# Query-key scores for 96 heads: float32 loads on the store queue with casts on GpSimd, in place of casting loads

## The chip, the cores and the metric

The kernel runs on one core of one Trainium2 chip. Its time is the device time of one execution, in microseconds. Differences of a few tenths of a per cent count here, so the profile of one execution is read beside the median of several.

## The reference

For 8 batches of 12 heads, every query row is multiplied with every key row. There is no scale, no mask and no softmax:

```
q, k: (8, 12, 1024, 64) float32
out = np.einsum('bhid,bhjd->bhij', q, k)      # (8, 12, 1024, 1024) float32
```

The inputs are 25.2 MB each, and the output is 402.7 MB. A head is one (1024 x 64) by (64 x 1024) product with 4 MB of output.

## The kernel before

The 96 heads are taken in batches of 1, 1, 2 and then 4 heads. For each batch, GpSimd's queue loads q and k from float32 in memory into float16 tiles (line 64); the DMA engines cast on the way. Three batches are loaded ahead and there are four input buffers.

A load of G heads puts 8 x G consecutive rows of the batch in each partition. TensorE transposes these rows through an identity (lines 78, 81, 82) so that the 64 head dimensions lie on partitions: for q, two tiles of rows side by side in one 128-column transpose; for k, each tile twice, to partitions 0-63 and 64-127, so that it meets either half of q. One such group, 4 + 16 transposes, goes to one PSUM tile (`t_ps`), and VectorE copies it out, q by head (line 91) and k in one copy (line 92).

`scores` makes one head: eight tiles of 128 query rows, each two products of 64 x 128 with 64 x 512 into a PSUM tile of two banks (`ps`, line 106; three such tiles). Tiles 1, 4 and 6 are evacuated by VectorE (line 112), the other five by ScalarE (line 114), into the head's output tile `o_sb` of 32 KB a partition. There are four of these. When all eight tiles are in, SP's queue stores the head in one 4 MB transfer (line 115), 32 KB per partition. A fifth head can therefore not be evacuated until the first one's store has landed.

Between the heads of a batch, the next batch is transposed. The order of instructions on each engine is set by the scheduler of the framework, which moved some products between the transposes; the queue of SP carries stores alone, and the queue of GpSimd carries loads alone.

Of the kernel before, what the change touches and what calls it, by code (L numbers as in the profile page):

```python
# [1 line left out]

# [5 lines left out]


F16 = mybir.dt.float16  # L10
F32 = mybir.dt.float32
P = 128


@with_exitstack
def kernel(
    ctx: ExitStack,
    tc: tile.TileContext,
    q: bass.AP,
    k: bass.AP,  # L20
    out: bass.AP,
):
    nc = tc.nc

    B, H, S, D = q.shape
    NT = S // P
    BH = B * H
    GMAX = 4
    assert D == 64 and NT == 8 and BH % GMAX == 0

    qf = q.rearrange("b h s d -> (b h s) d")
    kf = k.rearrange("b h s d -> (b h s) d")
    of = out.rearrange("b h i j -> (b h) i j")

    sizes = [1, 1, 2] + [GMAX] * (BH // GMAX - 1)
    assert sum(sizes) == BH  # L40

    consts = ctx.enter_context(tc.tile_pool(name="consts", bufs=1))
    ident = consts.tile([P, P], F16)

    in_pool = ctx.enter_context(tc.tile_pool(name="in_pool", bufs=4))
    tr_pool = ctx.enter_context(tc.tile_pool(name="tr_pool", bufs=2))
    out_pool = ctx.enter_context(tc.tile_pool(name="out_pool", bufs=4))
    pt_pool = ctx.enter_context(
        tc.tile_pool(name="pt_pool", bufs=1, space=bass.MemoryType.PSUM)
    )  # L50
    po_pool = ctx.enter_context(
        tc.tile_pool(name="po_pool", bufs=3, space=bass.MemoryType.PSUM)
    )

    class Batch:
        def __init__(self, first, G):
            self.first, self.G, self.R = first, G, 8 * G

        def load(self):
            rows = slice(self.first * S, (self.first + self.G) * S)  # L60
            self.q_sb = in_pool.tile([P, GMAX * NT, D], F16, tag="q")
            self.k_sb = in_pool.tile([P, GMAX * NT, D], F16, tag="k")
            for src, dst in ((qf, self.q_sb), (kf, self.k_sb)):
                nc.gpsimd.dma_start(  # L64
                    out=dst[:, : self.R],
                    in_=src[rows].rearrange("(p r) d -> p r d", p=P),
                )

        def alloc(self):
            self.qT = tr_pool.tile([P, GMAX * 4 * P], F16, tag="qT")  # L70
            self.kT = tr_pool.tile([P, GMAX * S], F16, tag="kT")

        def transpose(self, a):
            G, pp = self.G, P // self.G
            t_ps = pt_pool.tile([P, 12, P], F16, tag="pt")
            for e in range(4):
                r = a * NT + 2 * e
                nc.tensor.transpose(t_ps[:, e], self.q_sb[:, r : r + 2], ident)  # L78
            for t in range(NT):
                rows = self.k_sb[:, a * NT + t]  # L80
                nc.tensor.transpose(t_ps[0:64, 4 + t], rows, ident)  # L81
                nc.tensor.transpose(t_ps[64:128, 4 + t], rows, ident)  # L82
            qT = self.qT[:, : G * 4 * P].rearrange(
                "c (g e m a) -> c g e m a", g=G, e=4, m=pp
            )
            kT = self.kT[:, : G * S].rearrange(
                "c (g m a t) -> c g m a t", g=G, m=pp, t=NT
            )
            for g in range(G):
                ms = slice(g * pp, (g + 1) * pp)  # L90
                nc.vector.tensor_copy(out=qT[:, g, :, :, a], in_=t_ps[:, 0:4, ms])  # L91
            nc.vector.tensor_copy(  # L92
                out=kT[:, :, :, a],
                in_=t_ps[:, 4:12].rearrange("c t (g m) -> c g m t", g=G),
            )

        def scores(self, g):
            bh = self.first + g
            qT = self.qT.rearrange("c (g e m) -> c g e m", e=4, m=P)
            kT = self.kT.rearrange("c (g j) -> c g j", j=S)  # L100
            o_sb = out_pool.tile([P, NT, S], F32, tag="out")
            for t in range(NT):
                h = (t % 2) * 64
                ps = po_pool.tile([P, S], F32, tag="po")
                for n in range(2):
                    nc.tensor.matmul(  # L106
                        ps[:, n * 512 : (n + 1) * 512],
                        qT[h : h + 64, g, t // 2],
                        kT[h : h + 64, g, n * 512 : (n + 1) * 512],
                    )  # L110
                if t in (1, 4, 6):
                    nc.vector.tensor_copy(out=o_sb[:, t], in_=ps)  # L112
                else:
                    nc.scalar.copy(out=o_sb[:, t], in_=ps)  # L114
            nc.sync.dma_start(
                out=of[bh].rearrange("(p t) j -> p (t j)", p=P),
                in_=o_sb.rearrange("p t j -> p (t j)"),
            )

    batches, first = [], 0  # L120
    for G in sizes:
        batches.append(Batch(first, G))
        first += G

    AHEAD = 3
    for b in batches[:AHEAD]:
        b.load()
    make_identity(nc, ident)
    batches[0].alloc()
    for a in range(batches[0].G):  # L130
        batches[0].transpose(a)
    for i, b in enumerate(batches):
        if i + AHEAD < len(batches):
            batches[i + AHEAD].load()
        nxt = batches[i + 1] if i + 1 < len(batches) else None
        if nxt:
            nxt.alloc()
        for g in range(b.G):
            b.scores(g)
            if nxt:  # L140
                for a in range(g * nxt.G // b.G, (g + 1) * nxt.G // b.G):
                    nxt.transpose(a)


# [1 line left out]
_INS = ['q', 'k']  # L146
_OUTS = [((8, 12, 1024, 1024), 'float32')]


# [23 lines left out]
```

## Time and profile before

| what | value |
|---|---|
| median of 10 runs | 1071.07 us (1070.06 to 1071.59) |
| the profiled execution | 1071.11 us |
| span of its instructions | 1069.3 us |
| TensorE products and transposes, busy | 626.5 us, 3456 |
| VectorE busy | 566.0 us, 758 instructions |
| ScalarE busy | 468.5 us |
| GpSimd busy | 28.4 us |
| stores | 96 of 4 MB, median 36.6 us from issue to landing |
| casting loads | 52 |

The span is the time from the first to the last instruction in the profile. "Busy" is the time in which an engine executes; a share below one means that it waits for something. The time from issue to landing of a transfer includes its wait behind earlier transfers. The lines of the profile that carry the argument are shown in the prediction.

### The profile page before, as it was taken

To read this page: it belongs to the slowest core of one execution; us is meant where nothing else is said; L and a number is where in the kernel's file an instruction comes from. 1 tells how busy PE (TensorE), PEld (TensorE's weight loads), DVE (VectorE), ACT (ScalarE), POOL (GpSimd) and SP (SyncE) were. 2 spreads that over 40 slices of the span, in tenths; PEclk is the share of its full clock that TensorE was granted. 3 is DMA by queue.
4 is the path that set the end of the run, shared out by engine and by line. 5 is a ranking of instruction groups with operands and counts; after the bars stand their busy time and mean duration, and the time that the engine had idled before them with its cause. 6 is when DMAs were issued, how large, how long until landed. Compare 5 with 4: busy or idle time off the path is not lost.

```text
span 1069.3 us, 8844 instructions
## 1 busy us (share of the span) xinstructions
PE 626.5 (59%) x3456; PEld 213.2 (20%) x3456; DVE 566.0 (53%) x758; ACT 468.5 (44%) x481; POOL 28.4 (3%) x58
## 2 busy tenths in 40 slices
PE   6786565574755646556465565655655567667530
PEld 2222121121221212212122121121211212212100
DVE  5676455464554645536456465564654656655420
ACT  4454453444434444444444434444344445454530
POOL 3000000000000000000000000000000000000000
PEclk9985555555555555555555555555555555555555
DMA  9999999999999999999999999999999999999996
GB/s 203 389 386 391 391 406 415 387 421 401 402 420 389 417 402 398 419 389 415 406 398 423 386 409 409 398 423 387 409 410 398 421 434 430 430 430 431 431 433 288
DMA packets 21353, 428.39 MB, mean 401 GB/s; under 512 B 2368, under 2 KB 2880, under 8 KB 9024
## 3 DMA queue, kind: packets, MB, share of 16 engines
q1 hardware_dynamic: 13824, 402.66, 88.0%
q0 software_dynamic: 7488, 25.17, 11.9%
q8 instruction: 27, 0.44, 0.1%
q14 instruction: 14, 0.11, 0.0%
HBM read 50.33 MB, written 402.65 MB: 424 GB/s over the span
## 4 chain that ended last, share of the span: by engine, by line
DMA 77%; PE 7%; ACT 7%; DVE 1%; issue 0%; ACTq 0%
DMA out_dram<-o_sb 77%; ACT o_sb L114 7%; PE ps L106 6%; DVE kT L92 0%; DVE qT L91 0%; PE t_ps L81 0%; PE t_ps L78 0%; DVE o_sb L112 0%; PE t_ps L82 0%; ACTq L114 0%
## 5 line engine op out<-in xcount | busy, mean ns | idle before, releaser
L114 ACT COPY o_sb<-ps 128x1024 f32<-128x1024 f32 x480 | 467.2, 1014 | 566.2 <-DMA out_dram<-o_sb 345.4
L106 PE MATMUL ps<-kT,qT 64*128 64x512 f16 x1536 | 479.1, 595 | 272.6 <-ACT o_sb L114 228.8
L112 DVE COPY o_sb<-ps 128x1024 f32<-128x1024 f32 x288 | 352.0, 1224 | 372.1 <-DMA out_dram<-o_sb 210.2
L106 PEld LDWEIGHTS <-qT 64*128 64x128 f16 x1536 | 99.8, 109 | 604.1 <-issue 579.4
L91 DVE COPY qT<-t_ps 128x128 f16<-128x128 f16 (+1 forms) x374 | 121.3, 469 | 97.1 <-PE t_ps L82 97.0
L78 PE MATMUL t_ps<-ident,q_sb 128*128 128x128 f16 x384 | 56.7, 300 | 135.3 <-DVE kT L92 129.6
L92 DVE COPY kT<-t_ps 128x1024 f16<-128x1024 f16 x96 | 118.8, 1238 | 0.0
L81 PE MATMUL t_ps<-ident,k_sb 128*64 128x128 f16 x768 | 103.1, 312 | 0.0
L82 PE MATMUL t_ps<-ident,k_sb 128*64 128x128 f16 x768 | 102.9, 312 | 0.0
L81 PEld LDWEIGHTS <-k_sb 128*64 128x64 f16 x768 | 77.9, 166 | 19.9 <-issue 19.5
L82 PEld LDWEIGHTS <-k_sb 128*64 128x64 f16 x768 | 77.7, 165 | 8.4 <-issue 8.4
L78 PEld LDWEIGHTS <-q_sb 128*128 128x128 f16 x384 | 34.7, 127 | 187.9 <-issue 121.9
L64 POOL DMA_DIRECT2D q_sb<-in_q_dram x26 | 14.0, 539 | 767.0 <-PE t_ps L78 766.2
L64 POOL DMA_DIRECT2D k_sb<-in_k_dram x26 | 13.9, 536 | 13.2 <-PE t_ps L82 13.1
L114 ACT ACT_TABLE_LOAD x1 | 1.3, 1283 | 0.7 <-PEq L157 0.7
masks.py:199 POOL TENSOR_SCALAR_AFFINE_SELECT ident<-ident 128x128 f16<-128x128 f16 x1 | 0.4, 357 | 0.0
masks.py:197 POOL MEMSET ident<- 128x128 f16 x1 | 0.3, 267 | 0.0
L157 POOL MEMSET const-float32-0.0<- 128x1 f32 x1 | 0.1, 99 | 0.2 <-issue 0.2
L157 POOL MEMSET const-bfloat16-1.0<- 128x1 bf16 x1 | 0.1, 102 | 0.0
L157 POOL MEMSET const-uint8-127<- 128x1 uint8 x1 | 0.1, 102 | 0.0
L157 POOL MEMSET const-float32-1.0<- 128x1 f32 x1 | 0.1, 99 | 0.0
## 6 DMA issues: line engine op xcount, KB each, us to landing
out_dram<-o_sb SPq DMA_DIRECT2D x96, 4096.0 KB, 36.6
q_sb<-in_q_dram POOLq DMA_DIRECT2D x23, 512.0 KB, 17.9
k_sb<-in_k_dram POOLq DMA_DIRECT2D x23, 512.0 KB, 29.2
q_sb<-in_q_dram POOLq DMA_DIRECT2D x2, 128.0 KB, 3.6
k_sb<-in_k_dram POOLq DMA_DIRECT2D x2, 128.0 KB, 3.7
q_sb<-in_q_dram POOLq DMA_DIRECT2D x1, 256.0 KB, 5.1
k_sb<-in_k_dram POOLq DMA_DIRECT2D x1, 256.0 KB, 5.8
```

The lines of the kernel that those rows point to most:

```text
L64: nc.gpsimd.dma_start(out=dst[:, : self.R], in_=src[rows].rearrange("(p r) d -> p r d", p=P),)
L78: nc.tensor.transpose(t_ps[:, e], self.q_sb[:, r : r + 2], ident)
L81: nc.tensor.transpose(t_ps[0:64, 4 + t], rows, ident)
L82: nc.tensor.transpose(t_ps[64:128, 4 + t], rows, ident)
L91: nc.vector.tensor_copy(out=qT[:, g, :, :, a], in_=t_ps[:, 0:4, ms])
L92: nc.vector.tensor_copy(out=kT[:, :, :, a], in_=t_ps[:, 4:12].rearrange("c t (g m) -> c g m t", g=G),)
L106: nc.tensor.matmul(ps[:, n * 512 : (n + 1) * 512], qT[h : h + 64, g, t // 2], kT[h : h + 64, g, n * 512 : (n + 1) * 512],)
L112: nc.vector.tensor_copy(out=o_sb[:, t], in_=ps)
L114: nc.scalar.copy(out=o_sb[:, t], in_=ps)
L157: nc = _bacc.Bacc("TRN2", target_bir_lowering=False, num_devices=1)
```

## The change

Heads are taken in blocks of 2, 2, 4 and then 8, each in two halves of 1, 1, 2 and 4 heads. Each block is loaded in four pieces: q and k of the first half, q and k of the second. The pieces are plain float32 transfers, into three input buffers of 8 KB a partition. GpSimd casts each piece to float16 and places the two halves side by side in one block buffer (`half_sb`, one buffer): 64 columns of the first half, 64 of the second. One 128 x 128 transpose thus puts the first half's head dimensions on partitions 0-63 and the second half's on 64-127, for q and for k alike. A group is 8 transposes of q or 8 of k, to a PSUM tile of one bank (two of these), and one VectorE copy.

All instructions are held in the order in which they are written (`pin`). The transposes of the next block are written into the scores of the current one: q's after tile 1 and k's after tile 6, for as many heads as the next block has in a half.

At the start, the pieces of the first three blocks go to an output tile that is not yet in use, and three of the fourth block's pieces to the input buffers, from SP's and ScalarE's queues in turn. Later pieces are issued on SP's queue between the stores. `refill` does it: after the last head that transposes the next block, it casts three pieces of the block after that, loads and casts the fourth, and loads the first piece of yet another block; the other two follow after later heads. In the last block, two of the four pieces are cut by partition into several transfers.

```diff
-    in_pool = ctx.enter_context(tc.tile_pool(name="in_pool", bufs=4))
+    in_pool = ctx.enter_context(tc.tile_pool(name="in_pool", bufs=3))
+    half_pool = ctx.enter_context(tc.tile_pool(name="half_pool", bufs=1))
...
+            cuts = (0, P)
+            if self.first + 2 * self.G == BH and n < 2:
+                cuts = ((0, 112, 120, 124, 126, 127, P), (0, 112, 119, 124, 127, P))[n]
+            for lo, hi in zip(cuts, cuts[1:]):
+                pin(eng.dma_start(out=raw[lo:hi], in_=src[lo:hi]))
...
+        def cast(self, n):
+            pin(
+                nc.gpsimd.tensor_copy(
+                    out=self.halves[n % 2][:, :, n // 2],
+                    in_=self.raw[n].rearrange("p (r d) -> p r d", d=D),
+                )
+            )
...
+            for t in range(NT):
+                rows = self.halves[x][:, a * NT + t]
+                pin(nc.tensor.transpose(t_ps[:, t], rows, ident))
...
+                if t in side:
+                    side[t]()
...
+    for b in blocks[:3]:
+        for n in range(4):
+            piece = raw[:, 2 * at + n * b.elems :][:, : b.elems]
+            b.load(n, (nc.sync, nc.scalar)[n % 2], piece)
+        b.place(half_sb, at)
+        at += 2 * b.elems
+    for n in range(3):
+        blocks[3].load(n, (nc.sync, nc.scalar)[n % 2])
...
+    def refill(i):
+        b = blocks[i] if i < len(blocks) else None
+        c = blocks[i + 1] if i + 1 < len(blocks) else None
+        if b:
+            half_sb = half_pool.tile([P, 2 * half_elems], F16, tag="half")
+            b.place(half_sb, 0)
+            for n in range(3):
+                b.cast(n)
+            b.load(3, nc.sync)
+            b.cast(3)
+        if c:
+            c.load(0, nc.sync)
+        yield
+        if c:
+            c.load(1, nc.sync)
+        yield
+        yield
+        yield
+        if c:
+            c.load(2, nc.sync)
...
+        for n in range(2 * b.G):
+            side = {}
+            if nxt and n < nxt.G:
+                side = {
+                    1: lambda: nxt.transpose(n, 0),
+                    6: lambda: nxt.transpose(n, 1),
+                }
+            b.scores(n, side)
+            for job in todo:
+                next(job, None)
+            if nxt and n == nxt.G - 1 and i > 0:
+                todo.append(refill(i + 2))
+                next(todo[-1])
```

## The prediction

> **What bounds the kernel now.** I read the page's DMA lines first, then the queues and the chain, then the transfers of the store line, then stretches of time.
>
> ```profile
> DMA  9999999999999999999999999999999999999996
> q1 hardware_dynamic: 13824, 402.66, 88.0%
> q0 software_dynamic: 7488, 25.17, 11.9%
> HBM read 50.33 MB, written 402.65 MB: 424 GB/s over the span
> DMA 77%; PE 7%; ACT 7%; DVE 1%; issue 0%; ACTq 0%
> ```
>
> The 16 DMA engines are full in every slice but the last; the stores (q1) and the casting loads (q0) together fill them, and the chain that ends last is mostly stores. PE (59%), DVE (53%) and ACT (44%) have room. The chain, near the end, and the store line:
>
> ```profile
> 956.66 33.75 DMA out_dram<-o_sb
> 990.46 0.04 issue
> 990.50 1.02 ACT o_sb L114
> ...
> 995.17 1.02 ACT o_sb L114
> 996.21 33.44 DMA out_dram<-o_sb
> ...
> L115 SPq DMA_DIRECT2D out_dram<-o_sb x96: 332/332/366, 18.4 to 1035.5; - x96
> DMA to landing us min/median/max: 18.2/36.6/39.2
> ```
>
> A store lands and frees its output buffer, the next head takes 5.8 us (990.46 to 996.21), and its store waits behind three others. So compute has about three stores, 29 us, of cover, and only an empty store queue costs time. The drain, by stretches:
>
> ```profile
> 1040.00:1055.00 15.00, 0.00 (x0) 0.00 (x0) 0.00 (x0) 0.00 (x0) 0.00 (x0) 0.50 1.00 430
> 1055.00:1060.00 5.00, 0.00 (x0) 0.00 (x0) 0.00 (x0) 0.00 (x0) 0.00 (x0) 0.50 0.78 334
> 1060.00:1062.00 2.00, 0.00 (x0) 0.00 (x0) 0.00 (x0) 0.00 (x0) 0.00 (x0) 0.50 0.49 213
> 1062.00:1068.00 6.00, 0.00 (x0) 0.00 (x0) 0.00 (x0) 0.00 (x0) 0.00 (x0) 0.50 0.10 44
> ```
>
> The DMA share falls to 0.10 while the slowest engine still works: the engines finish unevenly. The trace's semaphore records give the sizes: the last store's 16 parts land from 1056.9 to 1068.7 us, mean 1061.6, so the slowest is 7.1 us behind the mean; at 122 us it was 1.4 us.
>
> **What the skill says.** "DMA: Bandwidth & Descriptors", Queues, rings and completion order: on each DMA engine the descriptors of one queue are consumed in ring order, and queues are taken in turn. The trace agrees for the turns: while loads are queued, store packets and load packets alternate. That a load on SP's queue waits behind all stores issued before it is what this prediction rests on; before has no such load. The same page, section on why a DMA increments by 16, says that a transfer over fewer partitions uses the lowest-numbered engines; no run here shows it yet. Prices from two further places stand below.
>
> **The change part by part.**
>
> *Loads.* The same 50.33 MB are read. Packet records of before: a 32 KB store packet steps every 1209.5 ns alone; a store and an 8 KB casting load together step 1526, so the load costs 316.5 ns; in the first 20 us, loads alone step 305. Before, per DMA engine: 48 x 305 + 320 x 316.5 ns + 5.1 us for the small batches = 121.0 us. After, float32 and not alternating, I take 305 ns: 352 x 305 ns + 10.0 us for the small blocks = 117.4. Gain 3.6 us; bounds 6 (full rate of a store packet, 302 ns and cheaper switches) and a loss of 8 (a turn from write to read costing some 0.15 us at each of about 56 transfers).
>
> *TensorE's instruction fetch.* 6912 PE instructions (3456 matmuls, 3456 loads of weights) are fetched in 27 pieces of 16 KB, each holding one DMA engine 0.9 us. After there are 4608, so 18 pieces: 9 x 0.9 / 16 = 0.5 us gained. PE, DVE (758 instructions to 384: 288 evacuations and 96 copies of about 1.2 us, where five copies of 0.47 to 1.24 us went) and ACT gain time too, worth nothing behind the stores' cover.
>
> *Last block's cut loads.* Partitions 112 to 127 go in small pieces; if those fall on low engines, engines 8 to 15 move 14 packets in place of 16 (0.6 us less) and engine 0 moves 23 (2.1 us more). Gain 0.6 if the slowest is a high one, loss 2 if it is a low one. The extra issues on SP, 9 at 0.33 us, lie under three queued stores.
>
> *Casts on GpSimd.* 14 blocks of four copies. MEMSET of 128 columns takes 267 ns and of one 99, so 1.3 ns a column: 2.7 us for 2048 columns, 0.8 for 512. The skill's "GPSIMD Engine Reference", section 3.1, has 1.8 cycles at 1.2 GHz per element for a tight loop: estimate 3.1 us; at one cycle it would be 1.8. I take 2.7. In the steady blocks, four casts, 11 us, fall in a block of about 87 us: hidden.
>
> *Where loads are behind stores.* From block 4 on a block has 8 heads and its successor's data lands four heads before it is transposed: hidden. In the short early blocks it is not. Number the heads from 0: block 0 has heads 0-1, block 1 2-3, block 2 4-7, block 3 8-15. The casts of block 3 start when head 3's last transposes release the half buffer, and only then is block 3's fourth piece loaded, on SP's queue behind store 3. Head 4 needs it: its eight transposes stand on PE ahead of its last product, so store 4 waits for it. Let T be the end of store 3. Load lands T + 2.5 (8 packets of 305 ns) + 0.5 (landing, as at the end of before); cast 2.7 -> T + 5.7; semaphore and transposes 1.1; last product 0.6; ACT copy 1.0 -> T + 8.4; issue to first packet 2.0 -> T + 10.4. Only block 4's first piece (2.5 us) is queued meanwhile, to T + 4.9. DMA idle: 5.5 us.
>
> Second time: block 4's third and fourth pieces are issued after store 7, and head 8 needs both, the first behind its second product. T' = end of store 7. Third piece lands T' + 3.0, cast T' + 5.7, transposes 6.8; DVE's qT copy (1.2) is ahead of its evacuations, ACT has three to make, and the sixth tile is produced at T' + 10.2; transposes, last product, ACT copy -> T' + 13.4 at half clock; first packet T' + 15.4. Queued meanwhile: three loads, to T' + 7.4. Idle: 8.0 us.
>
> The issue-to-packet time is the doubtful one. The skill's "DMA: Bandwidth & Descriptors", Latency and other measured facts, has 0.6 us to the first byte; the trace's first store is issued at 18.4 and its first packet starts at 23.0, 4.6 us later, but beside a full load queue. So 1.0 to 4.6; I take 2.0. With the cast from 1.8 to 3.5 the two stalls together are 9 to 20 us, I take 13.5.
>
> *Start.* First packet at 2.87 us before; I expect the same. 7.3 MB of loads are queued first: 8 x 0.65 + 4 x 1.25 + 3 x 2.45 = 17.6 us, to 20.4. The first head needs four landings (5.5), casts (8.5), transposes and two copies (11.0) and 7.5 us: issued at 18.5, first packet 20.5. Stall 0 to 3, I take 0.4.
>
> *Skew.* A stall lets all DMA engines start evenly again at about 125 us; that takes 1 us off the slowest.
>
> Sum: -3.6 - 0.5 - 0.6 - 1.0 + 13.5 + 0.4 = +8.2 us on the profiled span of 1069.3, whose run took 1071.11 us, equal to the median of 1071.07 within 0.1. So 1071.1 + 8.2 = 1079.
>
> **Rivals.** (1) Faster. The two early loads are in time, because they overtake the stores on the queue or arrive by another order than I read: then 13.9 us drop out and 1071.1 - 5.7 = 1065.4 is left. The stalls must fall under 3.6 us together for the kernel to be faster by 0.2%. For it: every steady block has its slack. Against: on SP the fourth piece stands after store 3, and one queue runs in order. (2) The 4.6 us issue time holds at every empty queue: 2.6 more at three places, 1079 + 8 = 1087. (3) Stalls at their short end, 9 us, with gains of 6 to 8: 1071 to 1074, no or little difference. (4) Loads cost more in one queue with the stores than alternating: 1079 + 8 to 12 = 1087 to 1091. Against: 13 ns per store packet is what alternating costs now.
>
> **How the numbers follow.** My forecast (1074 to 1084) has 0.45; (1), 1062 to 1069, 0.25; (3) 0.15; (2) and (4) together 0.15. A change under 0.2% (2.1 us) can't be told from none: same is 0.13, nearly all of (3). Slower is 0.45 + 0.15 = 0.60. Faster is 0.25 and the 0.02 of (3) in which the gains win: 0.27. The range takes 1063, leaving out the low end of (1), to 1087, leaving out the upper part of (2) and (4); the likeliest case alone is 1074 to 1084.
>
> **What would show it.** Right: in the DMA line two gaps of 5 to 8 us near 64 and 119 us; PE's transposes waiting for GpSimd's cast there, the cast for a load; full share afterwards; store period by head 9.7 us, 87 us a block; 18 fetches. Wrong: no gap before 130 us (rival 1); a longer period per block (rival 4); the gap from issue to packet at 4 us (rival 2); a slowest engine that is not 7 us behind at the end, since the cut then did more than I gave it.

## The result, and the profile after

The changed kernel takes 1091.41 us (median of 8 runs, 1089.02 to 1092.88) against 1071.05 us (29 runs) before. The ratio is 1.0186, with a 95% interval of 1.0177 to 1.0195: 20.4 us slower. The forecast was 1079 with a range to 1087, so its direction was right and its size was not. The profiled execution of the changed kernel, with a span of 1087.2 us and a time of 1089.02, is the fastest of the eight; sums over its trace therefore explain 17.9 us of span, and not the 20.4 between the medians.

From the page of the changed kernel, the lines that answer to those shown of before:

```profile
DMA  9989699999999999999999999999989999999997
q1 hardware_dynamic: 20912, 449.85, 97.2%
q8 instruction: 18, 0.29, 0.1%
HBM read 50.33 MB, written 402.65 MB: 417 GB/s over the span
DMA 72%; PE 20%; ACT 4%; POOL 0%; issue 0%; DVE 0%; SPq 0%; ACTq 0%
```

The same bytes move at 417 instead of 424 GB/s. The row of digits, one for each 27 us, now has holes: an 8 and a 6 in the third and fifth slices (54 to 82 us and 109 to 136 us) and an 8 in the thirtieth (788 to 815 us). PE's share of the chain that ends last has gone from 7% to 20%. The first two holes are the stalls that the prediction placed near 64 and 119 us, and the third is one that it did not have. TensorE's instructions are fetched in 18 pieces (q8), as worked out.

The chain of the changed kernel in its first part, start and duration in us, says how the two early stalls come about:

```profile
42.62 0.33 SPq L143
...
43.05 20.84 DMA x_sb<-in_k_dram
...
63.95 1.91 POOL half_sb L95
65.90 1.03 PE t_ps L110 x8
...
95.92 21.86 DMA x_sb<-in_q_dram
...
117.84 1.91 POOL half_sb L95
119.79 1.04 PE t_ps L110 x8
120.83 4.38 PE ps L135 x10
```

A load of 1 MB is issued right after a store and takes 20.8 us to land, a later one 21.9 us, because on one queue a load comes after the stores queued there. This is the order that the Trainium skill gives in "DMA: Bandwidth & Descriptors", Queues, rings and completion order, and the trace agrees. Then everything runs in series: cast, transposes, products. The timeline of the changed kernel from the second landing to the next store (start, duration, what; in brackets the idle time ahead and what ended it):

```profile
117.84 1.90 POOL L95 CAST half_sb<-x_sb 128x2048 f16<-128x2048 f32 x1 [20.53 <-DMA x_sb<-in_q_dram]
119.79 1.04 PE L110 MATMUL t_ps<-ident,half_sb 128*128 128x128 f16 x8 [23.01 <-POOL half_sb L95]
120.76 4.44 PE L135 MATMUL ps<-kT,qT 64*128 64x512 f16 x10
120.86 2.44 DVE L122 COPY qT<-t_ps 128x1024 f16<-128x1024 f16 x1 [22.76 <-PE t_ps L110]
...
128.21 0.34 SPq L143 DMA_DIRECT2D out_dram<-o_sb  x1
```

TensorE has stood still for 23.0 us when the transposes start. The ten products after them take 4.44 us, a step of 0.43 us from one to the next, where before the products of a row stepped 0.24 us on average, beside their partners on the other half of the partitions. From landing to the issue of the store it is 10.4 us; the store's first packet starts at 129.05.

What the 16 DMA engines do meanwhile is seen in stretches of time of the changed kernel. The columns are stretch, length, busy time of PE, PE's loads, DVE, ACT and POOL with counts, granted clock, DMA share, GB/s:

```profile
65.00:70.00 5.00, 4.10 (x19) 1.96 (x20) 1.53 (x2) 1.93 (x2) 0.84 (x1) 1.00 0.27 113
120.00:129.00 9.00, 9.00 (x35) 3.59 (x34) 6.08 (x5) 4.76 (x5) 1.90 (x1) 1.00 0.07 27
793.00:799.00 6.00, 3.17 (x8) 1.01 (x7) 2.02 (x2) 2.04 (x3) 0.00 (x0) 1.00 0.57 216
1060.00:1079.00 19.00, 0.00 (x0) 0.00 (x0) 0.00 (x0) 0.00 (x0) 0.00 (x0) 1.00 1.00 431
1079.00:1082.00 3.00, 0.00 (x0) 0.00 (x0) 0.00 (x0) 0.00 (x0) 0.00 (x0) 1.00 0.31 131
1082.00:1087.00 5.00, 0.00 (x0) 0.00 (x0) 0.00 (x0) 0.00 (x0) 0.00 (x0) 1.00 0.05 20
```

The first three lines are the three holes: at 120 to 129 us all compute engines are at work and the DMA engines have nothing. The last three are the drain after the last product. (The granted clock is 1.00 in this execution and 0.52 in two others; these took 1091.04 and 1090.08 us, inside the range of the rest.)

The packet records of both traces give a ledger. Idle time is that of all 16 engines together, divided by 16; how the smallest gaps are counted moves such sums, here and in the runs below, by up to 1.1 us and their differences by up to 0.7:

| us | before | after | difference |
|---|---|---|---|
| start | 3.0 | 2.0 | -1.0 |
| two early gaps | 0 | 4.8 + 8.4 | +13.2 |
| gap at 793 to 798 us | 0 | 3.2 | +3.2 |
| drain | 7.6 | 6.1 | -1.5 |
| all idle time, the above and small gaps | 10.8 | 25.2 | +14.4 |
| packets under way | 1058.5 | 1062.0 | +3.5 |
| span | 1069.3 | 1087.2 | +17.9 |

The last three rows close. The third gap is read from the chain of the changed kernel between 757 and 798 us:

```profile
757.25 3.57 PE ps L135 x8
...
762.81 1.00 ACT o_sb L139
763.81 0.02 issue
763.83 34.04 DMA out_dram<-o_sb
797.87 0.02 issue
797.89 0.03 SPq L143
```

and from SP's own timeline of it:

```profile
764.25 0.95 SPq L82 DMA_DIRECT2D x_sb<-in_k_dram  x1
765.68 22.58 SPq L82 DMA_DIRECT2D x_sb<-in_q_dram  x6
797.95 0.38 SPq L143 DMA_DIRECT2D out_dram<-o_sb  x1
800.37 5.72 SPq L82 DMA_DIRECT2D x_sb<-in_k_dram  x5
```

SP does not wait for data here: the store at 797.95 is issued when the store of 763.83 has landed. Between the two stand seven transfers, one whole piece and the six parts of a cut one, so the second store is the eighth transfer after the first. The parts themselves take 22.58 us to issue instead of six times 0.33, waiting in the same manner for the stores before. The trace's records of SP's instructions say why. Each transfer reports its completion on a semaphore (a counter that other instructions can wait for), SP's transfers use eight of these in turn, and before each issue SP waits for the semaphore that this transfer is going to use. The stores of 763.83 and 797.95 have one semaphore in common; the store of 744.06 and the fifth part, issued at 778.23, have another. An issue thus waits until the transfer eight places back has landed. The prediction counted the parts at 0.33 us each and did not ask what their issue waits for.

### The profile page after: what moved, and what is told of

Its sections match the earlier page's. It is cut to its first block, busy times and chain, and to the rows that moved or that the text cites. A ratio compares the mean times of both kernels' runs of the same rounds, so it can differ in the third digit from the quotient of the medians.

```text
span 1087.2 us, 6274 instructions
## 1 busy us (share of the span) xinstructions
PE 759.5 (70%) x2304; PEld 272.3 (25%) x2304; DVE 507.9 (47%) x384; ACT 476.4 (44%) x481; POOL 91.8 (8%) x62
## 4 chain that ended last, share of the span: by engine, by line
DMA 72%; PE 20%; ACT 4%; POOL 0%; issue 0%; DVE 0%; SPq 0%; ACTq 0%
DMA out_dram<-o_sb 67%; PE ps L135 17%; ACT o_sb L139 4%; PE t_ps L110 3%; DMA x_sb<-in_q_dram 2%; DMA x_sb<-in_k_dram 2%; POOL half_sb L95 0%; DMA early<-in_q_dram 0%; DVE o_sb L137 0%; DVE kT L122 0%; ACTq L139 0%; SPq L143 0%; SPq L82 0%
## 5 line engine op out<-in xcount | busy, mean ns | idle before, releaser
L135 PE MATMUL ps<-kT,qT 64*128 64x512 f16 x1536 | 672.8, 624 | 248.1 <-ACT o_sb L139 245.0
L139 ACT COPY o_sb<-ps 128x1024 f32<-128x1024 f32 x480 | 475.1, 1013 | 570.0 <-DMA out_dram<-o_sb 308.5
L135 PEld LDWEIGHTS <-qT 64*128 64x128 f16 x1536 | 198.1, 136 | 655.6 <-issue 653.2
L95 POOL CAST half_sb<-x_sb 128x2048 f16<-128x2048 f32 x44 | 82.3, 1896 | 794.2 <-PE t_ps L110 473.0
L110 PE MATMUL t_ps<-ident,half_sb 128*128 128x128 f16 x768 | 99.2, 311 | 45.5 <-POOL half_sb L95 45.5
L122 DVE COPY qT<-t_ps 128x1024 f16<-128x1024 f16 x48 | 110.7, 2306 | 31.9 <-PE t_ps L110 31.9
L110 PEld LDWEIGHTS <-half_sb 128*128 128x128 f16 x768 | 74.2, 141 | 124.3 <-issue 75.3
L122 DVE COPY kT<-t_ps 128x1024 f16<-128x1024 f16 x48 | 58.3, 1215 | 14.1 <-PE t_ps L110 14.1
L95 POOL CAST half_sb<-early 128x512 f16<-128x512 f32 (+1 forms) x12 | 8.8, 758 | 5.6 <-DMA early<-in_q_dram 5.4
```

The lines of the kernel that those rows point to most:

```text
L95: nc.gpsimd.tensor_copy(out=self.halves[n % 2][:, :, n // 2], in_=self.raw[n].rearrange("p (r d) -> p r d", d=D),)
L110: pin(nc.tensor.transpose(t_ps[:, t], rows, ident))
L122: pin(nc.vector.tensor_copy(out=dst, in_=src))
L135: pin(nc.tensor.matmul(ps[:, js], qT[cs, g, t], kT[cs, g, js]))
L139: pin(nc.scalar.copy(out=o_sb[:, t], in_=ps))
```

## The experiments

Where 8.2 us were forecast, 20.4 were measured. The theories after the result were that the two late pieces cost the 13 us of their gaps (A) and the cut pieces of the last block another 3 to 5 (C). The rivals were that products which have lost their partners set TensorE's pace (B), and dearer packets all through the run.

**1. Take the lateness away.** The two blocks whose pieces come late cast pieces that have long landed, so some of their scores are made from other rows. The loads are still issued and waited for by nobody in these places.

```diff
+        def cast(self, n, of=None):
...
-                    in_=self.raw[n].rearrange("p (r d) -> p r d", d=D),
+                    in_=self.raw[n if of is None else of].rearrange("p (r d) -> p r d", d=D),
...
-            for n in range(3):
-                b.cast(n)
+            b.cast(0)
+            b.cast(1)
+            b.cast(2, 0 if i == 4 else None)
             b.load(3, nc.sync)
-            b.cast(3)
+            b.cast(3, 1 if i in (3, 4) else None)
```

> The late pieces of the fourth and fifth block (fourth piece; third and fourth piece) are still loaded, but their casts read the block's first pieces, which landed long before; the scores of these two blocks are therefore those of other rows. Theory A (these pieces lie behind store 3 and store 7 in SP's queue, and the store queue runs dry while they are waited for): the DMA gaps of 4.8 us at 65-70 us and of 8.4 us at 120-129 us both go, 1091.4 - 13 = 1078 us. Rival B (TensorE's products, which are slower in the changed kernel, set the pace, and the gaps are where that shows): less than 4 us is gained, above 1087 us, and gaps open elsewhere.

Measured: 1073.45 us (10 runs), ratio to before 1.0023 (1.0013 to 1.0032). That is 18.0 us less than the changed kernel. Stretches of time of this run, with the columns as above:

```profile
60.00:70.00 10.00, 9.44 (x46) 4.11 (x45) 9.02 (x8) 6.24 (x7) 0.00 (x0) 0.88 1.05 406
115.00:130.00 15.00, 7.67 (x26) 2.69 (x25) 5.11 (x5) 5.17 (x6) 2.65 (x2) 0.50 1.00 429
775.00:783.00 8.00, 5.12 (x13) 1.73 (x12) 3.49 (x3) 3.31 (x4) 0.00 (x0) 0.50 0.57 223
```

Both early holes are closed, and the third is still there, earlier by what was gained. So the late pieces are 18.0 of the 20.4 us, and not 13. In the two traces the difference is 16.3: idle time falls by 13.2 (25.2 to 12.0), and the packets take 3.1 less (1062.0 to 1058.9). Behind the first store after each early hole of the changed kernel, the 8 KB load packets take 460 ns on average (80.1 to 84.5 us) and 466 ns (139.3 to 143.8 us), where the median is 309: eight packets on each engine, 1.2 us each time. That store's last packets, begun at 78 and 137.5 us, take 1.95 us in place of 1.21. An idle queue thus costs more than the idle time.

**2. Leave the last block uncut.** The pieces of the last block go in one transfer each; the late pieces stay.

```diff
-            if self.first + 2 * self.G == BH and n < 2:
+            if False:
```

> The two cut pieces of the last block are loaded whole. Theory C (the nine extra transfers wait in SP's order for the completion of earlier stores, because each transfer takes the semaphore of the one eight before it, and the stores behind them are issued late): the DMA gap of 3.3 us at 793-799 us goes and half of the slow load packets beside it, 1091.4 - 3 to 5 = 1087 us; the drain at the end may lengthen by up to 1.5 us. Rival D (the gap belongs to the last loads however they are cut): no change within 1 us, or slower by the longer drain.

Measured: 1088.28 us (4 runs), 1.0157 (1.0140 to 1.0174), 3.1 us less than the changed kernel. The gap at 793 us is gone. The drain goes from 6.1 to 11.6 us, more than the 1.5 us that was expected: the gap had let the DMA engines start evenly again, and without it the slowest ends 10.8 us behind the mean of the 16, where it was 5.3 in the changed kernel. Run 9 below, whose parts load all engines alike and which keeps the gap, ends with 4.2, against 10.8 in run 3; so it is the gap that does this, and not the shares of the parts.

**3. Both at once.** The edits of 1 and 2.

```diff
-            if self.first + 2 * self.G == BH and n < 2:
+            if False:
...
+            b.cast(2, 0 if i == 4 else None)
...
+            b.cast(3, 1 if i in (3, 4) else None)
```

> Both edits of the two experiments before together, with the same rows left out. Theories A and C: the gains add, 1091.4 - 13 - 4 = 1074 us, within 1 us of the sum of the two. Rival B: 1085 us or more. If it stays above 1071 us, what is left over the kernel before is not an empty queue but dearer packets.

Measured: 1071.61 us (12 runs), 1.0004 (0.9996 to 1.0013): not told from before. The queue is never empty between start and drain. Against before, the packets take 2.2 us less (1056.3), the start 0.8 less, and the drain 3.2 more. Its end, in stretches of time of this run:

```profile
1040.00:1055.00 15.00, 0.00 (x0) 0.00 (x0) 0.00 (x0) 0.00 (x0) 0.00 (x0) 0.50 0.96 415
1055.00:1060.00 5.00, 0.00 (x0) 0.00 (x0) 0.00 (x0) 0.00 (x0) 0.00 (x0) 0.50 0.38 164
1060.00:1065.00 5.00, 0.00 (x0) 0.00 (x0) 0.00 (x0) 0.00 (x0) 0.00 (x0) 0.50 0.17 72
1065.00:1069.90 4.90, 0.00 (x0) 0.00 (x0) 0.00 (x0) 0.00 (x0) 0.00 (x0) 0.50 0.03 13
```

For 15 us only some of the engines work. The whole 20.4 us now has its parts: 18.0 from the late pieces (changed kernel less run 1), 1.8 from the cut (run 1 less run 3), and 0.6 for everything else (run 3 less before), which is within what can be measured. Taken in the other order, over run 2, the cut is 3.1 and the late pieces are 16.7: the two share 1.3 us.

**4. The lost pairing alone, in the kernel before.** All products read partitions 0 to 63, so that neighbours no longer use different halves.

```diff
-                h = (t % 2) * 64
+                h = 0
```

> The kernel before, with all products on TensorE's partitions 0-63: the odd tiles of query rows are then those of the even tiles, and nothing else is left out. In the profile of before the products of neighbouring tiles, on different halves of TensorE's rows, step every 0.23 us; in the changed kernel, where a head lies in one half, every 0.44 us. Theory F (the lost pairing costs nothing while three stores are queued): a head takes 8 us in place of 5.8, the DMA share stays full, 1071 us within 1. Rival B (slower products set the pace wherever they are): 1076 us or more.

Measured: 1070.86 us (12 runs), 0.9999 (0.9990 to 1.0007). TensorE's line of its page, against 626.5 (59%) of before:

```profile
PE 821.3 (77%) x3456; PEld 328.0 (31%) x3456; DVE 569.6 (53%) x758; ACT 476.9 (45%) x481; POOL 28.3 (3%) x58
```

In this kernel the products now step 0.43 us, as in the changed kernel (its expectation has 0.23 for the 0.24 of before, and 0.44). The 194.8 us more of TensorE cost nothing while the stores cover them. The price falls due only where the queue is empty, as in the ten products at 120.76 us above.

**5. Later loads on GpSimd's queue.** The changed kernel, uncut, with the four loads of `refill` moved off SP; nothing else is left out.

```diff
-            b.load(3, nc.sync)
+            b.load(3, nc.gpsimd)
...
-            c.load(0, nc.sync)
+            c.load(0, nc.gpsimd)
...
-            c.load(1, nc.sync)
+            c.load(1, nc.gpsimd)
...
-            c.load(2, nc.sync)
+            c.load(2, nc.gpsimd)
```

> All loads after the first fifteen are issued on GpSimd's queue in place of SP's, without a cast in the transfer, and the last block is not cut; nothing is left out. Theory A: they take turns with the stores in place of standing behind them, land within 10 us, and the gaps at 65 and 120 us go: 1091.4 - 13.2 - 3.3 = 1075 us, about 3 us dearer for turns (316 ns a packet in place of 309) and 2 to 3 us cheaper because no load runs beside the start of a single store: 1073 to 1078 us. Rival B: 1085 us or more. Rival E (what the SP queue lost is lost in any queue, since the loads are the same bytes at the same time): no change.

Measured: 1076.86 us (4 runs), 1.0051 (1.0036 to 1.0066), 11.4 us less than run 2. The second gap is gone and the first is still 3.9 us. The timeline of this run has the load and the cast that waits for it:

```profile
46.45 0.67 POOL L82 DMA_DIRECT2D x_sb<-in_k_dram  x1
...
62.96 1.89 POOL L95 CAST half_sb<-x_sb 128x2048 f16<-128x2048 f32 x1 [15.84 <-DMA x_sb<-in_k_dram]
```

Even in a queue of its own the load takes 16.4 us, where less than 10 was expected. Its first packet starts 5.1 us after the issue, at 51.5 us. From there the queues are taken in turn, as the same section of the skill says, but a turn of the store queue is a 32 KB packet of 1.21 us, and one of the load queue 8 KB, about 0.31 us. On each engine the piece is eight packets, so from the first to the end of the last it is about 7 x 1.52 + 0.31 = 11.0 us. Overtaking helps only if the load is issued early enough for both.

**6. and 7. A cut store in the kernel before.** Since the cut had levelled the engines in the changed kernel, one store of the kernel before is cut by partitions: head 84, and then heads 76 and 86.

```diff
-            nc.sync.dma_start(
-                out=of[bh].rearrange("(p t) j -> p (t j)", p=P),
-                in_=o_sb.rearrange("p t j -> p (t j)"),
-            )
+            dst = of[bh].rearrange("(p t) j -> p (t j)", p=P)
+            src = o_sb.rearrange("p t j -> p (t j)")
+            cuts = (0, 112, 120, 127, P) if bh in (84,) else (0, P)
+            for lo, hi in zip(cuts, cuts[1:]):
+                nc.sync.dma_start(out=dst[lo:hi], in_=src[lo:hi])
```

> The kernel before; the store of head 84 goes in four transfers, of partitions 0-111, 112-119, 120-126 and 127. Theory H (the drain is long because one DMA engine is slower, the slow one is in the upper half, and pieces over few partitions fall on the lowest engines): engines 8-15 move one 32 KB packet less, 1.2 us, the end comes 1.2 us earlier, 1070 us. Rival I (the slow engine is a low one, or pieces fall elsewhere): no gain, or 1.2 to 5 us more.

> As the run with one store cut, with the stores of heads 76 and 86 cut. Theory H: twice the gain, 2.4 us, 1068.7 us. Rival I: no gain, or 2.4 to 10 us more.

Measured: 1086.89 us (4 runs), 1.0137 (1.0107 to 1.0166), and with two cut stores 1103.63 us (4 runs), 1.0302 (1.0242 to 1.0363). Each costs 16 us or more, where a gain of 1.2 us or a loss of at most 5 was expected; the levelling that was hoped for did not come. Stretches of time of the run with one:

```profile
940.00:950.00 10.00, 8.49 (x26) 1.49 (x23) 4.80 (x4) 6.51 (x7) 0.00 (x0) 0.50 1.01 328
950.00:960.00 10.00, 0.04 (x1) 0.04 (x2) 1.08 (x1) 1.10 (x2) 0.00 (x0) 0.50 1.03 282
960.00:980.00 20.00, 9.83 (x76) 4.61 (x76) 11.86 (x23) 3.76 (x4) 0.00 (x0) 0.50 0.98 365
```

The DMA engines are fully busy and move only 328, 282 and 365 GB/s: packets take up to 4.66 us in place of 1.21. Against the 430 of undisturbed stores that is 10 x (1 - 328/430) + 10 x (1 - 282/430) + 20 x (1 - 365/430) = 8.8 us. The drain grows from 7.6 to 17.0 us, another 9.4; together 18.2. This execution is the slowest of the four, with a span of 1088.2 us, and 18.9 us above the span before is what there is to explain.

**8. Is it the number of transfers or their few partitions?** The same store in four transfers of a quarter of the columns each, over all 128 partitions.

```diff
+            cuts = (0, 2048, 4096, 6144, 8192) if bh in (84,) else (0, 8192)
+            for lo, hi in zip(cuts, cuts[1:]):
+                nc.sync.dma_start(out=dst[:, lo:hi], in_=src[:, lo:hi])
```

> The kernel before; the store of head 84 goes in four transfers by columns, each over all 128 partitions, 8 KB a partition. Rival L (the 16 us of the run with a store cut by partition come from transfers over a few partitions, which load few DMA engines and slow the packets beside them): 1071 us, within 1. Rival M (any store in four transfers costs it): 1080 us or more.

Measured: 1071.96 us (12 runs), 1.0008 (0.9999 to 1.0016). Four transfers cost nothing that can be told from zero; the 16 us come with the cut by partitions. The landings in the trace of run 6 say more. The store ahead of the cut one lands on its first engine at 941.2 us, the part over 112 partitions at 950.0 and the first of the small parts at 951.2. One queue is served in order, so the slow packets from 940 to 950 us are there before any small part is: the part over 112 partitions is slow too. No run has this part without the small ones. By the skill, "DMA: Bandwidth & Descriptors", section on why a DMA increments by 16, the number of engines is the largest up to 16 that divides the partitions, and they are the lowest-numbered. So the parts use 16, 8, 7 and 1 engines, and the trace agrees in the number: the run of head 84 has 13840 packets on this queue instead of 13824, and 8 + 7 + 1 = 16 is what three more transfers with one closing packet on each of their engines give. Engine 0 gets seven, one, one and one data packets of this store, ten in place of eight, or 2.4 us more. That is a small part of the 16, and the part over 112 partitions uses all 16 engines; why packets of 1.21 us grew to 4.66 stays open.

**9. The same question for the cut loads.** Run 1 with the last block's two pieces cut by columns, again in six and five transfers.

```diff
-                cuts = ((0, 112, 120, 124, 126, 127, P), (0, 112, 119, 124, 127, P))[n]
+                cuts = ((0, 384, 768, 1152, 1472, 1792, 2048), (0, 448, 832, 1216, 1664, 2048))[n]
...
-                pin(eng.dma_start(out=raw[lo:hi], in_=src[lo:hi]))
+                pin(eng.dma_start(out=raw[:, lo:hi], in_=src[:, lo:hi]))
```

> The run with early data, with the same rows left out; the last block's two pieces are cut into the same number of transfers, six and five, but by columns, so that each goes over all 128 partitions. Theory C (the transfers wait for the semaphore of the one eight before, whatever they carry): the gap of 3.8 us near 776-782 us stays, 1073.5 us. Rival L (transfers over a few partitions are what is slow): the gap goes, 1071.6 us, as without the cut.

Measured: 1072.44 us (20 runs), 1.0013 (1.0007 to 1.0020), 1.0 less than run 1. SP's timeline and the stretch of the gap in this run:

```profile
750.64 22.33 SPq L82 DMA_DIRECT2D x_sb<-in_q_dram  x6
782.39 0.34 SPq L143 DMA_DIRECT2D out_dram<-o_sb  x1
```

```profile
775.00:780.00 5.00, 5.00 (x13) 1.78 (x12) 2.45 (x2) 2.87 (x3) 0.00 (x0) 1.00 0.57 227
```

The number of transfers has stayed and so has the gap, 4.4 us of it; their shape has changed. For the gap it is the count that matters, as the eight semaphores say. The time lies between those of run 1 and run 3, whose difference is 1.8 us: 0.8 of it have stayed with the count, and 1.0 went with the shape.

**10. and 11. Smaller blocks, loaded two blocks ahead.** The halves have two heads instead of four, there are eight input buffers, all pieces of a block are requested two blocks before they are cast, and nothing is cut. The edit is shown for SP's queue (run 10); in run 11 the four loads of `d` name `nc.gpsimd` instead.

```diff
-    GMAX = 4
+    GMAX = 2
...
-    sizes = [1, 1, 2] + [GMAX] * (BH // (2 * GMAX) - 1)
+    sizes = [1, 1] + [GMAX] * (BH // (2 * GMAX) - 1)
...
-    in_pool = ctx.enter_context(tc.tile_pool(name="in_pool", bufs=3))
+    in_pool = ctx.enter_context(tc.tile_pool(name="in_pool", bufs=8))
...
-        c = blocks[i + 1] if i + 1 < len(blocks) else None
+        d = blocks[i + 2] if i + 2 < len(blocks) else None
...
-            for n in range(3):
+            for n in range(4):
                 b.cast(n)
-            b.load(3, nc.sync)
-            b.cast(3)
...
+        if d:
+            d.load(0, nc.sync)
+            d.load(1, nc.sync)
         yield
+        if d:
+            d.load(2, nc.sync)
+            d.load(3, nc.sync)
```

> The changed kernel with blocks of 4 heads in place of 8 (after two blocks of 2), eight input buffers of half the size, so that every piece is loaded two blocks ahead and none is waited for behind a store; the last block is not cut; nothing is left out. Theory A: no gap in the DMA share between 10 and 1050 us, as in the run with early data and no cut, 1071.6, and about 1.5 us more for load packets of 4 KB (159 ns in place of half of 309): 1071 to 1074 us. Rival G (what that run gained came from the rows left out): above 1080 us.

> The small blocks of the run before, with all later loads on GpSimd's queue in place of SP's, still float32 and cast by GpSimd; nothing is left out. In the runs so far the slowest DMA engine ended 11 us behind the mean with 1 MB loads on SP's queue, 15 us with twice as many of half the size, and 7 us with loads on GpSimd's queue. Theory J (loads on the store queue are what one DMA engine falls behind with): it ends 7 us behind, 1080.8 - 9 + 1 to 3 us for load packets that take turns with stores = 1073 to 1075 us. Rival K (it is the number of small transfers that does it, on whatever queue): 15 us behind, 1080 us or more.

Measured: 1080.84 us (4 runs), 1.0095 (1.0062 to 1.0129), on SP's queue, where 1071 to 1074 was expected; 1072.87 us (20 runs), 1.0016 (1.0009 to 1.0022), on GpSimd's. With SP's queue no gap is left, but the drain takes 16.5 us, with the slowest engine 15.3 us behind the mean. Its end in stretches of time:

```profile
1060.00:1065.00 5.00, 0.00 (x0) 0.00 (x0) 0.00 (x0) 0.00 (x0) 0.00 (x0) 1.00 0.36 157
1065.00:1070.00 5.00, 0.00 (x0) 0.00 (x0) 0.00 (x0) 0.00 (x0) 0.00 (x0) 1.00 0.21 92
1070.00:1075.00 5.00, 0.00 (x0) 0.00 (x0) 0.00 (x0) 0.00 (x0) 0.00 (x0) 1.00 0.17 72
1075.00:1080.00 5.00, 0.00 (x0) 0.00 (x0) 0.00 (x0) 0.00 (x0) 0.00 (x0) 1.00 0.06 26
```

On GpSimd's queue the drain is 10.4 us and the slowest engine 9.2 behind, where 7 was expected if the queue decides and 15 if the number of small transfers does. This run computes every score and comes within 1.3 us of run 3, so what run 3 gains does not come from the rows that it leaves out. It is the fastest version that keeps the change's float32 loads and computes everything: 18.5 us faster than the changed kernel, and still 0.16% slower than before. No version was found that beats the kernel before. That agrees with its profile: its DMA engines never idle between start and drain, so only a cheaper packet or a more even end could beat it.

## Why the prediction was right and wrong

**Late pieces: the mechanism and the idle time were right, the term was short.** Expected were 5.5 + 8.0 us of idle DMA; the trace has 4.8 + 8.4. That the sum is so close is partly luck. The issue to first packet was taken as 2.0 us and is 0.84 at each of these stores (68.97 to 69.81, 128.21 to 129.05). The cast was taken as 2.7 us and is 1.90; with the 1.8 cycles of the skill's "GPSIMD Engine Reference", section 3.1, it would be the 3.1 that the prediction names, and the measurement decides for 1.1 cycles a column at that page's 1.2 GHz. That is near the 1.03 cycles which the same section has for the smallest loop bodies and which the prediction passed over. Against these, q's copy took 2.44 us where 1.2 was written down, and ten products took 4.44 us. The prediction said of TensorE only that it gains time, "worth nothing behind the stores' cover". Run 4 confirms the cover. But a head that lies in one half of the partitions takes a product every 0.43 us, and in a stall that counts. (The skill's "TensorEngine Tiling (Array Packing)", Key Properties, has tiles on different partitions work in parallel; the steps of 0.24 us before and 0.43 after agree.) What the sum lacked altogether is what comes after an empty queue: 3.1 us of dearer packets in the two traces. By medians the term is 18.0 instead of 13.5; 1.7 us of that is not found in the traces compared, of which the changed kernel's is its fastest execution.

**The last block's cut: wrong.** The step that failed is "The extra issues on SP, 9 at 0.33 us, lie under three queued stores". They wait for the stores, the six parts hold SP for 22.58 us, and the next store is late: 3.2 us of idle queue in the place of a gain of 0.6. The net cost, run 1 less run 3, is 1.8, because the same gap lets the engines start evenly again and shortens the drain; reckoned over run 2 it is 3.1.

**Loads and skew: wrong, and the largest error.** The steps that failed are "I take 305 ns" for a load packet and "A stall lets all DMA engines start evenly again at about 125 us; that takes 1 us off the slowest". Without late data or cuts, the packets cost 2.2 us less than before, where the prediction had 3.6 for loads and 0.5 for fetches. The mean load packet in run 3 is 319 ns, not 305: in one queue with the stores a load costs about what it cost in turn with them, 316.5. The 0.15 us for a turn from writing to reading, in the prediction's bound, were assumed; what run 3 shows is less, since the 10 ns by which this mean lies above the median come to 0.08 us over the eight packets of a piece. The skew was to shrink by 1.0; in run 3 the slowest engine is 10.8 us behind instead of 7.1, and the drain 3.2 us longer. Run 3 has no stall, but run 2 has both, and its slowest engine is 10.8 us behind too: what starts evenly at 125 us has fallen behind again by the end. With the start, these items were to bring -3.6 - 0.5 - 1.0 + 0.4 = -4.7 us, and run 3 less before is +0.6. That is an error of 5.3 us (4.2 of it from the drain and 1.9 from the packets, while the start came out 1.2 better), larger than the 4.5 of the late pieces and the 2.4 of the cut; together they are the 12.2 between the +8.2 of the sum and the +20.4 measured.

**The rivals.** Rival 1, loads that overtake the stores, is excluded by the chain. Rival 2, 4.6 us from issue to packet, is excluded by the 0.84 (and the 4.6 itself is 4.4, since the packet times of the prediction are some 0.24 us late: the first store of before is issued at 18.37 us, and its first packet starts at 22.74). Rival 3, stalls of 9 us and gains of 6 to 8, is excluded by the 13.2 us of gaps and by run 3, which gains nothing over before. Rival 4, dearer loads in one queue, is right only near the empty queues: the mean load packet is 330 ns in the changed kernel. The range ended at 1087, because it gave the failing cases one cause each; the short gains, the longer term and the third gap came together.

**What stays open.** Three things were seen and not explained. Why the slowest DMA engine falls further behind when the loads are on the store queue: 7.1 us before, 6.8 with loads on GpSimd's queue (run 5), 10.8 with them on SP's (run 3); with more and smaller ones it is 9.2 on GpSimd's queue (run 11) and 15.3 on SP's (run 10). Why load packets are slow behind the first store after an empty queue: all engines read at once there, but they do so at the start of the changed kernel too, from 13 to 20 us, with packets of 314 ns. And why a transfer cut by partitions, the part over 112 included, has slow packets.

## What to carry to other kernels

A load that is moved onto a queue of large stores must be asked for as early as the stores queued ahead of it take, not as early as the load takes; and in a queue of its own, for as many turns of a store packet as it has packets on an engine, and the wait for its first packet besides (5.1 us in run 5). Before splitting a transfer, count the transfers between it and the stores on the issuing engine, since an issue can wait for a transfer several places back, eight in this program. Work that is free under cover is priced again for each place where the cover is gone.

## What the runs showed of the hardware

Cutting one 4 MB store among 96 by partitions (112, 8, 7, 1) cost 16 us, and by columns nothing that can be told from zero. The first packet of a store on an idle queue starts 0.84 us after its issue begins, at two places, and 0.87 at a third where a few packets were still under way. GpSimd casts 2048 columns of float32 to float16 in 1.90 us. Load packets of 8 KB that take 309 ns at the median take 460 and 466 behind the first store after an empty queue. SP issued a transfer only when the transfer with the same semaphore, eight places back, had landed: 22.58 us for six parts of a load.
